# The turned part of the latent heads' keys: two zero-padded tiles of 128 rows in place of one of twice 64 rows

## The chip, the cores and the metric

The kernel runs on one core of a Trainium2 chip, in one launch. Time is the device time of a whole execution in microseconds (us), the median over several runs. A profiled execution has a time of its own; its span runs from the first instruction to the last.

The engines are named as in the profile: PE multiplies matrices (PEld is its loading of weights, which runs beside the multiplying), DVE and ACT work elementwise, POOL too, and SP issues the transfers.

## What is computed

One step of a two-layer transformer for two groups of 128 tokens each, a prompt and a sample; the sample also sees a cache of 128 tokens. The first layer has eight latent heads (multi-head latent attention) and eight grouped-query heads, the second differential attention; each layer has a gated feed-forward part with a convolution of width 3, and modulation vectors from a condition. What matters here is the latent heads. Their key has two parts: 128 features of the head's own, made from a compressed vector, and 64 features that all eight heads share, which are turned by the token's position (rotary embedding):

```python
k_rope = apply_rope(k_rope[:, :, None, :], cos_r, sin_r)[:, :, 0]
krope_all = jnp.concatenate([ctx[1], k_rope], axis=1)
kv = (ckv_all @ w_kv_up).reshape(b, s, MLA_HEADS, MLA_NOPE_DIM + MLA_V_DIM)
ka = jnp.concatenate(
    [kv[..., :MLA_NOPE_DIM], jnp.broadcast_to(krope_all[:, :, None, :], (b, s, MLA_HEADS, MLA_ROPE_DIM))],
    axis=-1)
out_a = softmax_attention(jnp.concatenate([qa_nope, qa_rope], axis=-1), ka, va, MLA_SCALE)
```

A score is therefore a sum over 128 + 64 features. For the prompt there is no cache and no turn.

## The kernel before

**Layout.** Features stand on the 128 rows (partitions) of a tile, tokens along the columns: columns 0 to 127 are the prompt (group 0), then the sample. Keys have three such blocks: prompt, cache, sample. Weights come as blocks of 128 x 128 from memory in transfers of 1 MB (`raw`) and are split by ACT into a rounded high part (`wh`, line 220) and by DVE into the rest (`wl`, line 221); each product is then three matmuls (lines 313, 314, 317). Scores, transposes and attention sums are plain fp32 matmuls, which PE executes in two steps each.

**The turned key.** The weights are arranged so that the 64 shared features are computed twice: row 10 of `pr` (the product of the input with `w_in_ab`, tile name proj) holds them on rows 0 to 63 and again on rows 64 to 127. The cached ones arrive doubled in the same way. The tile `kr` has 128 rows and the three blocks of 128 columns:

- `caches()` (lines 647 to 653) loads the cached block, among the other caches, at the start of the last quarter of the input product (about 142 us).
- `key_rope()` (line 696), started once product 10 of that quarter is done (about 197 us), copies the prompt's block on ACT (line 697), sends it out as a result (line 698) and turns the sample's block on DVE straight into `kr` (line 699; `rope` has four quarter-row products, line 584, and two steps over all rows, lines 586 and 587).

**The queries' turned part.** `qr` is one tile for two heads: the even head's 64 features on rows 0 to 63, the odd head's on rows 64 to 127.

**The heads.** In the loop over `h`, PE makes the queries of two heads (three products) every second round, and in every round the head's keys `kn` and values. A grouped-query head and a latent head are started as generators: `head_ab` first puts the scores into one bank, then the softmax runs on DVE and ACT, and at later calls of `pump` come the transposes of the probabilities (`transposed`, line 607) and the sums (lines 631 to 633). Between these, PE has the products of the following heads and the modulation's rows (`sum_rows`, line 427, with 32 columns of weights). A latent head's scores take four matmuls: for each group the product with `kn` over 128 rows, then that with `kr` over the head's 64 rows:

```python
half = slice(64 * (h % 2), 64 * (h % 2) + 64)
return head_ab(hp, [(qnh, knh), (qrh[half], kr[half])], rsm,
               lambda b: vh[:, b], o, h)
```

A grouped-query head has one product for each group and so two matmuls (`kg`, `qb`).

**What sets the order.** The program is written as one stream and a scheduler places it on the engines; each engine then runs its list strictly in order, and waits are semaphores. Some transfers, those of the caches among them, are kept in the order of the program. Tiles of a pool lie one behind another in the order of their first use: behind `kr` in the pool `ab` stand `kg`, `vg`, `ql`, `qb` and the rest.

Of the kernel before, what the change touches and what calls it, by code (L numbers as in the profile page):

```python
# [18 lines left out]
P = 128  # L19
D = 2048  # L20
KD = D // P
T = 128
# [62 lines left out]
def step_kernel(ctx: ExitStack, tc: tile.TileContext, A: dict):  # L85
    nc = tc.nc
    pe, dve, act, pool, sp = nc.tensor, nc.vector, nc.scalar, nc.gpsimd, nc.sync
# [16 lines left out]
    def nm(s):  # L104
        uid[0] += 1
        return f"{s}_{uid[0]}"

    def T_(pl, shape, tag, dt=F32, bufs=None):
        kw = {} if bufs is None else {"bufs": bufs}
        return pl.tile(shape, dt, tag=tag, name=nm(tag), **kw)  # L110
# [8 lines left out]
    def C(name):  # L119
        a, w = _AT[name]  # L120
        return cst[:, a:a + w]
# [454 lines left out]
    def rope(dst, src, heads, half, cn, sn):  # L576

        cb = C(cn)[:, None, :].to_broadcast([P, heads, T])
        sn_ = C(sn)
        t = T_(tmp, [P, 2, T], "rope", bufs=1)  # L580
        for a in range(0, P, 2 * half):
            lo, hi = slice(a, a + half), slice(a + half, a + 2 * half)
            for to, of in ((hi, lo), (lo, hi)):
                dve.tensor_tensor(out=t[to, :heads], in0=src[of],
                                  in1=sn_[of, None, :].to_broadcast([half, heads, T]), op=ALU.mult)
        dve.tensor_tensor(out=dst, in0=src, in1=cb, op=ALU.mult)
        dve.tensor_tensor(out=dst, in0=dst, in1=t[:, :heads], op=ALU.add)
# [16 lines left out]
    def transposed(pl, p):  # L604
        pt = T_(ppool["att"], [P, 512], "att", bufs=3)
        for b in range(3):
            pe.transpose(pt[:, b * T:(b + 1) * T], p[:, b * T:(b + 1) * T], ident)  # L607
        o = T_(pl, [P, 3 * T], "pT", bufs=2)
        act.copy(o, pt[:, :3 * T])
        return o  # L610

    def head_ab(pl, pairs, rs, v, hx, c):

        s = T_(ppool["att"], [P, 512], "att", bufs=3)
        for g, ks in ((0, slice(0, T)), (1, slice(T, 3 * T))):
            for i, (q, k) in enumerate(pairs):
                pe.matmul(s[:, ks], q[:, g * T:(g + 1) * T], k[:, ks],  # L617
                          start=(i == 0), stop=(i == len(pairs) - 1))
        mx = T_(small, [P, 2], "mx")
        sums = T_(small, [P, 2], "sums")  # L620
        p = T_(pl, [P, 3 * T], "p", bufs=2)
        softmax_parts(s, mx, sums, rs, None, p)
        rec = T_(small, [P, 2], "rec")
        dve.reciprocal(out=rec, in_=sums)
        dve.tensor_scalar(out=p[:, :T], in0=p[:, :T], scalar1=rec[:, 0:1], scalar2=None, op0=ALU.mult)
        dve.tensor_scalar(out=p[:, T:], in0=p[:, T:], scalar1=rec[:, 1:2], scalar2=None, op0=ALU.mult)
        yield
        pT = transposed(pl, p)
        yield
        o = T_(ppool["att"], [P, 512], "att", bufs=3)  # L630
        pe.matmul(o[:, 0:T], v(0), pT[:, 0:T], start=True, stop=True)
        pe.matmul(o[:, T:NT], v(1), pT[:, T:2 * T], start=True, stop=False)
        pe.matmul(o[:, T:NT], v(2), pT[:, 2 * T:], start=False, stop=True)
        split(hx[:, c, :NT], hx[:, c, NT:2 * NT], o[:, :NT])


    def mixer_ab(hx, rb0, st):
        l = 0
        with tc.tile_pool(name="ab", bufs=1) as ab:
            with tc.tile_pool(name="abp", bufs=1) as pj:  # L640
                T_(ab, [P, SHIFT // 4], "pad")
                kv_in = T_(ab, [P, 4, 2, 3 * T], "kv_in", F32R)
                ckc = T_(pj, [P, 4, T], "ckc")
                kr = T_(ab, [P, 3 * T], "kr")
                kg = T_(ab, [P, 2, 3 * T], "kg")
                vg = T_(ab, [P, 3, 2, P], "vg")

                def caches():
                    tc.keep_in_program_order(sp.dma_start(out=ckc, in_=A["cache_ckv"]))
                    split(kv_in[:, :, 0, T:2 * T], kv_in[:, :, 1, T:2 * T], ckc)  # L650
                    tc.keep_in_program_order(sp.dma_start(out=kr[:, T:2 * T], in_=A["cache_krope"]))
                    tc.keep_in_program_order(sp.dma_start(out=kg[:, :, T:2 * T], in_=A["cache_gqa_k"]))
                    tc.keep_in_program_order(sp.dma_start(out=vg[:, 1], in_=A["cache_gqa_v"]))

# [4 lines left out]
                rsm = T_(ab, [P, 2], "rsmla")  # L659
                pr = T_(pj, [P, 15, NT], "proj")  # L660
# [33 lines left out]
                        sp.dma_start(out=A["o_ckv"], in_=ck[:, :, 0:T])  # L694

                def key_rope():
                    act.copy(kr[:, 0:T], pr[:, 10, 0:T])
                    sp.dma_start(out=A["o_krope"], in_=kr[0:64, 0:T])
                    rope(kr[:, None, 2 * T:], pr[:, 10:11, T:], 1, 32, "rcm", "rsm")
                    yield  # L700

                def keys(c):
# [88 lines left out]
            with tc.tile_pool(name="abh", bufs=1) as hp:  # L791
                ada["pew"] = PEW["heads"]

                o = T_(keep, [P, KD, ROW], "hx", F32R)
                load_cw(0)
                WQ = Weights(A["w_q_up"], 6, 2)
                WK = Weights(A["w_kv_up"], 4, 4)
                qh, qlo = (lambda k: ql[:, k, :NT]), (lambda k: ql[:, k, NT:])
                kh, klo = (lambda k: kv_in[:, k, 0]), (lambda k: kv_in[:, k, 1])
                qn, qr = {}, None  # L800

                def gqa_query(h):
                    s2 = T_(tmp, [P, NT], "sq", bufs=2)
                    act.activation(s2, qb[:, h], AF.Square)
                    act.activation(qb[:, h], qb[:, h], AF.Identity, scale=C("gqn"))
                    yield
                    pst = T_(pmisc, [P, 512], "misc")
                    for g in range(2):
                        pe.matmul(pst[:, g:g + 1], s2[:, g * T:(g + 1) * T], inv(128),
                                  start=True, stop=True)  # L810
                    rstd([pst[:, 0:2]], 2, HEAD_SCALE, rsb[:, h])
                    rope(qb[:, h:h + 1, T:], qb[:, h:h + 1, T:], 1, 64, "rch", "rsh")

                def gqa(h):
                    k = kg[:, h // 4]
                    return head_ab(hp, [(qb[:, h], k)], rsb[:, h], lambda b: vg[:, b, h // 4], o, 8 + h)

                def mla(h, qnh, qrh, knh, vh):
                    half = slice(64 * (h % 2), 64 * (h % 2) + 64)
                    return head_ab(hp, [(qnh, knh), (qrh[half], kr[half])], rsm,  # L820
                                   lambda b: vh[:, b], o, h)

                flush()
                start(gqa_query(0))
                for h in range(8):
                    if h % 2 == 0:
                        for i in range(2):
                            ps = gemm(WQ.chunk(), qh, qlo)
                            qn[h + i] = T_(hp, [P, NT], "qn", bufs=4)
                            act.copy(qn[h + i], ps)  # L830
                            pump(RATE["heads"])
                        ps = gemm(WQ.chunk(), qh, qlo)
                        ev = T_(tmp, [P, NT], "nt", bufs=4)
                        act.copy(ev, ps)
                        qr = T_(hp, [P, NT], "qr", bufs=2)
                        act.copy(qr[:, 0:T], ev[:, 0:T])
                        rope(qr[:, None, T:], ev[:, None, T:], 1, 32, "rcm", "rsm")
                        pump(RATE["heads"])
                    if h < 7:
                        start(gqa_query(h + 1))  # L840
                    start(gqa(h))
                    ps = gemm(WK.chunk(), kh, klo, 3 * T)
                    kn = T_(hp, [P, 3 * T], "kn", bufs=2)
                    act.copy(kn, ps)
                    pump(RATE["heads"])
                    ps = gemm(WK.chunk(), kh, klo, 3 * T)
                    vt = T_(hp, [P, 3 * T], "vt", bufs=2)
                    act.copy(vt, ps)
                    pump(RATE["heads"])

                    def values_and_head(h, vt, *a):
                        pt = T_(ppool["att"], [P, 512], "att", bufs=3)
                        for b in range(3):
                            pe.transpose(pt[:, b * T:(b + 1) * T], vt[:, b * T:(b + 1) * T], ident)
                        vm = T_(hp, [P, 3, P], "vm", bufs=2)
                        act.copy(vm.rearrange("p b d -> p (b d)"), pt[:, :3 * T])
                        yield
                        yield from mla(h, *a, vm)

                    start(values_and_head(h, vt, qn[h], qr, kn))  # L860
                flush()
# [370 lines left out]
```

## Time and profile before

| what | value |
| --- | --- |
| median of 3 runs | 2375.56 us (2375.53 to 2375.99) |
| profiled execution | 2375.77 us |
| its span | 2374.0 us, mean granted clock 0.989 |
| first and last scores of the latent heads | 246.5 and 363.5 us |
| their stage, from the first score of a grouped-query head | 228.0 to 363.6 us |
| memory traffic over the span | 257 GB/s on average |

How to read a row of the views. A group of instructions names line, engine, operation, tiles as written<-read, the form (for PE, rows*columns of the array, then rows x columns of the moving tile) and the count, then busy time and mean duration. In a timeline a row has its start, its duration and, in brackets, the idle time of its engine before it and what ended that. PE's matmuls are pipelined, so its rows overlap: what a matmul costs is the distance from its start to the next start, not its duration. An x2 is two steps merged into one row.

### The profile page before, as it was taken

The page shows a single profiled execution, that of the slowest core. Times are in us where ns is not written, and L with a number is a line of the kernel's source. Part 1 is how long each engine was busy: PE and PEld are TensorE (multiplying, and loading weights), DVE is VectorE, ACT ScalarE, POOL GpSimd, SP SyncE. Part 2 cuts the span into 40 slices and gives each one's busy share as a digit, 9 for nine tenths or more (in the row PEclk, how much of TensorE's full clock was granted, in tenths as well). Part 3 has the DMA queues.
Part 4 walks back from the last instruction along what each step waited for, and adds up shares of the span by engine and source line. Part 5 has one row for each costly group of instructions (what it writes and reads, how often), then busy time and mean ns, then how long its engine had stood idle before and what let it go on. Part 6 is the DMA issues. An engine that isn't in the chain of part 4 may idle for free.

```text
span 2374.0 us, 47094 instructions
## 1 busy us (share of the span) xinstructions
PE 2315.6 (98%) x19626; PEld 2196.9 (93%) x19626; DVE 1799.1 (76%) x2677; ACT 1172.7 (49%) x1855; POOL 136.6 (6%) x132
## 2 busy tenths in 40 slices
PE   8899999999999999999999999998999999999997
PEld 6778868799999999999989999897999999999997
DVE  2667544479999999999968889799899755666654
ACT  4345544365554345554465555445555434555542
POOL 0001001110000000001220000022000000000011
PEclk9999999999999999999999999998999999999998
DMA  9886677877767876777767788776677555555553
GB/s 378 353 342 241 238 266 300 309 275 266 261 252 281 296 277 251 265 264 268 300 229 256 267 315 290 269 288 240 247 260 260 207 195 195 196 194 192 192 192 120
DMA packets 92405, 610.81 MB, mean 257 GB/s; under 512 B 9952, under 2 KB 17824, under 8 KB 20512
## 3 DMA queue, kind: packets, MB, share of 16 engines
q1 hardware_dynamic: 92192, 607.80, 69.6%
q8 instruction: 154, 2.52, 0.4%
q14 instruction: 59, 0.48, 0.1%
HBM read 603.01 MB, written 4.75 MB: 256 GB/s over the span
## 4 chain that ended last, share of the span: by engine, by line
PE 95%; DVE 2%; DMA 1%; issue 1%; ACT 1%; POOL 0%; POOLq 0%; DVEq 0%; ACTq 0%
PE acc L313 28%; PE acc L317 28%; PE acc L314 28%; PE ada L427 3%; DMA araw<-w_ada 1%; PE att L617 1%; PE acc L300 1%; PE acc L299 1%; PE acc L301 1%; PE misc L427 0%; PE att L934 0%; PE att L607 0%; DVE wl L221 0%; PE ada L340 0%; PE ada L376 0%
## 5 line engine op out<-in xcount | busy, mean ns | idle before, releaser
L220 ACT CAST wh<-raw 128x1024 fp32r<-128x1024 f32 (+1 forms) x788 | 794.0, 1013 | 943.1 <-PE acc L314 775.7
L221 DVE TENSOR_TENSOR wl<-raw,wh 128x1024 fp32r<-128x1024 f32 (+1 forms) x788 | 923.0, 1186 | 343.8 <-ACT wh L220 324.5
L313 PE MATMUL acc<-hx,wh 128*128 128x256 f32 x4064 | 1131.6, 279 | 9.7 <-ACT wh L220 4.2
L317 PE MATMUL acc<-hx,wl 128*128 128x256 f32 x4064 | 1127.8, 278 | 0.7 <-DVE wl L221 0.7
L314 PE MATMUL acc<-hx,wh 128*128 128x256 f32 x4064 | 1128.4, 278 | 0.0
L313 PEld LDWEIGHTS acc<-hx,wh 128*128 128x128 f32 x4064 | 764.7, 188 | 35.7 <-issue 13.3
L317 PEld LDWEIGHTS acc<-hx,wl 128*128 128x128 f32 x4064 | 765.0, 188 | 8.9 <-issue 6.7
L314 PEld LDWEIGHTS acc<-hx,wh 128*128 128x128 f32 x4064 | 765.3, 188 | 7.4 <-issue 6.9
L404 DVE CUSTOM_DVE_ANT_0 junk<-araw,condb 128x2048 f32<-128x2048 f32 (+1 forms) x184 | 424.8, 2309 | 1.1 <-DMA araw<-w_ada 1.1
L314 PE MATMUL acc<-g,wh 128*128 128x256 f32 x1408 | 388.3, 276 | 0.0
L317 PE MATMUL acc<-g,wl 128*128 128x256 f32 x1408 | 388.0, 276 | 0.0
L313 PE MATMUL acc<-g,wh 128*128 128x256 f32 x1408 | 387.8, 276 | 0.0
L314 PEld LDWEIGHTS acc<-g,wh 128*128 128x128 f32 x1408 | 264.3, 188 | 0.0
L317 PEld LDWEIGHTS acc<-g,wl 128*128 128x128 f32 x1408 | 264.2, 188 | 0.0
L313 PEld LDWEIGHTS acc<-g,wh 128*128 128x128 f32 x1408 | 264.1, 188 | 0.0
L175 POOL TENSOR_TENSOR sqacc<-sqacc,sq 128x256 f32<-128x256 f32 x62 | 80.7, 1302 | 1584.3 <-issue 1290.8
L1011 ACT ACTIVATE cv<-acc,convw 128x256 f32<-128x256 f32 x176 | 98.3, 559 | 2.8 <-PE acc L301 2.8
L569 DVE SCALAR_TENSOR_TENSOR x<-acc,mod,x 128x128 f32<-128x128 f32 x192 | 58.0, 343 | 49.2 <-PE acc L317 49.2
L427 PE MATMUL ada<-araw,condw 128*32 128x512 f32 x608 | 83.2, 624 | 6.0 <-DMA araw<-w_ada 5.0
L1017 DVE SCALAR_TENSOR_TENSOR cv<-acc,convw,cv 128x254 f32<-128x254 f32 x176 | 84.4, 480 | 3.7
L1014 DVE SCALAR_TENSOR_TENSOR cv<-acc,convw,cv 128x254 f32<-128x254 f32 x176 | 83.7, 476 | 2.2 <-ACT cv L1011 2.2
L313 PE MATMUL acc<-oall,wh 128*128 128x256 f32 x208 | 58.4, 281 | 2.3 <-DVE x L569 2.3
(229 smaller groups left out, 1789.8 us busy)
## 6 DMA issues: line engine op xcount, KB each, us to landing
araw<-w_ada SPq DMA_DIRECT2D x186, 1024.0 KB, 5.4
raw<-w_up SPq DMA_DIRECT2D x176, 1024.0 KB, 4.8
raw<-w_down SPq DMA_DIRECT2D x88, 1024.0 KB, 4.8
raw<-w_in_c SPq DMA_DIRECT2D x48, 1024.0 KB, 5.5
raw<-w_in_ab SPq DMA_DIRECT2D x19, 1024.0 KB, 7.1
raw<-w_out_ab SPq DMA_DIRECT2D x16, 1024.0 KB, 7.1
raw<-w_out_c SPq DMA_DIRECT2D x16, 1024.0 KB, 5.3
raw<-w_ada SPq DMA_DIRECT2D x6, 1024.0 KB, 10.8
```

What stands on the lines that cost most here:

```text
L175: pool.tensor_tensor(out=st["acc"], in0=st["acc"], in1=sq, op=ALU.add)
L220: pin(act.copy(out_hi, src))
L221: pin(dve.tensor_tensor(out=out_lo, in0=src, in1=out_hi.bitcast(F32), op=ALU.subtract))
L313: fixed(pe.matmul(ps[:, :n], wh, xh(k), start=(i == 0), stop=False))
L314: fixed(pe.matmul(ps[:, :n], wh, xl(k), start=False, stop=False))
L317: fixed(pe.matmul(ps[:, :n], wl, xh(k), start=False, stop=(i == last)))
L404: tc.keep_in_program_order(dve.tensor_tensor_reduce(out=junk, in0=raw, in1=condb[:, c].rearrange("p (g n) -> p g n", g=4), scale=1.0, scal ...
L427: i = pe.matmul(ada["ps"][32 * g:32 * g + 32, :], condw[:, 4 * t + g, :], raw[:, g], start=(t == 0), stop=(t == 3), skip_group_check=True)
L569: dve.scalar_tensor_tensor(out=x[:, c, s], in0=ps[:, s], scalar=mod[:, l, 3 * which + 2, c, g:g + 1], in1=x[:, c, s], op0=ALU.mult, op1=AL ...
L1011: pin(act.activation(y, ps, AF.Identity, scale=cw[:, 1, m:m + 1], bias=cw[:, 3, m:m + 1]))
L1014: pin(dve.scalar_tensor_tensor(out=y3[:, :, 1:], in0=p3[:, :, :T - 1], scalar=cw[:, 0, m:m + 1], in1=y3[:, :, 1:], op0=ALU.mult, op1=ALU.add))
L1017: pin(dve.scalar_tensor_tensor(out=y3[:, :, :T - 1], in0=p3[:, :, 1:], scalar=cw[:, 2, m:m + 1], in1=y3[:, :, :T - 1], op0=ALU.mult, op1=A ...
```

## The change

`kr` becomes two tiles side by side, each of 128 rows: in the first, rows 0 to 63 hold the shared features and rows 64 to 127 are zero; in the second it is the other way round. POOL clears both once. Each half is filled separately: two transfers for the cached block, two copies on ACT for the prompt's, and the turn goes into a tile of its own (`turned`), from which two more copies on ACT fill the sample's block. In the scores, the whole of `qr` meets the tile of the head's parity: the other head's features meet zeros. The sums are the same.

```diff
-                kr = T_(ab, [P, 3 * T], "kr")
+                kr = T_(ab, [P, 2, 3 * T], "kr")
+                pool.memset(kr, 0.0)
+                halves = (slice(0, 64), slice(64, P))
...
-                    tc.keep_in_program_order(sp.dma_start(out=kr[:, T:2 * T], in_=A["cache_krope"]))
+                    for i, half in enumerate(halves):
+                        tc.keep_in_program_order(sp.dma_start(out=kr[half, i, T:2 * T], in_=A["cache_krope"][half]))
...
                 def key_rope():
-                    act.copy(kr[:, 0:T], pr[:, 10, 0:T])
-                    sp.dma_start(out=A["o_krope"], in_=kr[0:64, 0:T])
-                    rope(kr[:, None, 2 * T:], pr[:, 10:11, T:], 1, 32, "rcm", "rsm")
+                    for i, half in enumerate(halves):
+                        act.copy(kr[half, i, 0:T], pr[half, 10, 0:T])
+                    sp.dma_start(out=A["o_krope"], in_=kr[0:64, 0, 0:T])
+                    turned = T_(pj, [P, 1, T], "turned")
+                    rope(turned, pr[:, 10:11, T:], 1, 32, "rcm", "rsm")
+                    for i, half in enumerate(halves):
+                        act.copy(kr[half, i, 2 * T:], turned[half, 0])
                     yield
...
                 def mla(h, qnh, qrh, knh, vh):
-                    half = slice(64 * (h % 2), 64 * (h % 2) + 64)
-                    return head_ab(hp, [(qnh, knh), (qrh[half], kr[half])], rsm,
+                    return head_ab(hp, [(qnh, knh), (qrh, kr[:, h % 2])], rsm,
                                    lambda b: vh[:, b], o, h)
```

On PE and DVE the lists keep their instructions and their order. ACT, SP and POOL get a few more. ACT around the key's copies, before (line 697 copies the prompt's block, 220 rounds weights, 704 squares the grouped-query keys):

```order
L171 ACTIVATE sq_2036<-proj_240 128x256
L697 COPY kr_233<-proj_240 128x128
L220 CAST wh_2246<-raw_2240 128x1024
L704 ACTIVATE sq_2088<-proj_240 128x256
L704 ACTIVATE sq_2124<-proj_240 128x256
```

and of the change (lines 701 and 706 are the two pairs of copies, 711 is the former 704):

```order
L171 ACTIVATE sq_2038<-proj_241 128x256
L701 COPY kr_233<-proj_241 64x128 x2
L220 CAST wh_2252<-raw_2246 128x1024
L706 COPY kr_233<-turned_2061 64x128 x2
L711 ACTIVATE sq_2094<-proj_241 128x256
L711 ACTIVATE sq_2130<-proj_241 128x256
```

The second pair stands behind the rounding of weights and ahead of the squares; it waits for DVE's turn. SP around the cached block, before (lines 649 to 653 are the caches, 445 the modulation's weights, 265 the layer's weights):

```order
L649 DMA ckc_232<-cache_ckv 128x512
L651 DMA kr_233<-cache_krope 128x128
L445 DMA araw_1501<-w_ada 128x2048
L652 DMA kg_234<-cache_gqa_k 128x2x128
L653 DMA vg_235<-cache_gqa_v 128x256
L265 DMA raw_1799<-w_in_ab 128x2048
```

and of the change (lines 651 to 656 are the caches):

```order
L651 DMA ckc_232<-cache_ckv 128x512
L654 DMA kr_233<-cache_krope 64x128
L445 DMA araw_1502<-w_ada 128x2048
L654 DMA kr_233<-cache_krope 64x128
L655 DMA kg_235<-cache_gqa_k 128x2x128
L656 DMA vg_236<-cache_gqa_v 128x256
L265 DMA raw_1801<-w_in_ab 128x2048
```

The second half stands behind a transfer of modulation weights, ahead of the other caches and the next weights.

## Prediction

> **What bounds the kernel now.** I read the page first, then the busy times of the stage that the change touches, then PE's waits there, then single rows. On the page, the busy line and the chain that ended last:
>
> ```profile
> PE 2315.6 (98%) x19626; PEld 2196.9 (93%) x19626; DVE 1799.1 (76%) x2677; ACT 1172.7 (49%) x1855; POOL 136.6 (6%) x132
> ...
> PE 95%; DVE 2%; DMA 1%; issue 1%; ACT 1%; POOL 0%; POOLq 0%; DVEq 0%; ACTq 0%
> ```
>
> PE holds 95% of the chain: what PE is spared, where it does not wait for another, comes off the end. The stretches (start:end, length, then busy time of PE, PEld, DVE, ACT, POOL with their instructions, granted clock, DMA share, GB/s): the attention heads stand in the first, the output product behind them in the second.
>
> ```profile
> 228.00:363.60 135.60, 133.67 (x919) 102.02 (x918) 66.04 (x199) 69.80 (x164) 4.90 (x7) 1.00 0.69 258
> 380.00:400.00 20.00, 20.00 (x171) 17.11 (x170) 9.89 (x16) 7.85 (x10) 4.96 (x5) 1.00 0.99 397
> ```
>
> In the heads PE works 133.67 of 135.60 us at full granted clock; DVE and ACT work about half, DMA 0.69. All 1.9 us of PE's idle time there have these two names (total, times, longest):
>
> ```profile
> PE att L607 <- DVE p L625: 1.4, 2, 0.8
> PE ada L427 <- DVE mod L378: 0.5, 1, 0.5
> ```
>
> So this is a PE stage, and the question is what the scores cost on PE beyond their columns. The instructions of the score line, durations as minimum/median/maximum, first and last start:
>
> ```profile
> L617 PEld LDWEIGHTS att<-kn,qn x32: 186/189/192, 246.5 to 362.6; 128*128 128x128 f32 x32
> L617 PEld LDWEIGHTS att<-kr,qr x32: 182/184/186, 246.9 to 363.3; 64*128 64x128 f32 x32
> L617 PE MATMUL att<-kr,qr x32: 272/374/480, 246.9 to 363.5; 64*128 64x128 f32 x16, 64*128 64x256 f32 x16
> ```
>
> The 32 kr matmuls run with the array in the form 64*128: two fp32 steps for each of 16 matmuls, in 8 heads. A weight load takes as long with 64 rows (184 ns) as with 128 (189), so nothing is saved now by half the rows. The second latent head, PE in order of time:
>
> ```profile
> 259.03 0.39 PE L633 MATMUL att<-pT,vm 128*128 128x128 f32 x2
> 259.26 0.39 PE L617 MATMUL att<-kn,qn 128*128 128x128 f32 x2
> 259.57 0.49 PE L617 MATMUL att<-kr,qr 64*128 64x128 f32 x2
> 259.99 0.70 PE L617 MATMUL att<-kn,qn 128*128 128x256 f32 x2
> 260.62 0.70 PE L617 MATMUL att<-kr,qr 64*128 64x256 f32 x2
> 261.24 0.44 PE L317 MATMUL acc<-kv_in,wl 128*128 128x384 f32 x1
> 261.52 0.34 PE L313 MATMUL acc<-kv_in,wh 128*128 128x384 f32 x1
> 261.69 0.34 PE L314 MATMUL acc<-kv_in,wh 128*128 128x384 f32 x1
> ```
>
> Durations overlap in this view; the distance from start to start is the cost. L633, a pair of 128 columns in one array form, takes 259.26-259.03 = 0.23 us. The pairs that touch kr take 0.31, 0.42, 0.63 and 0.62, and the instruction behind them, 384 columns, takes 0.28 where its like takes 0.17. For the 256-column pair without a change of form, a grouped-query head, whose four steps are one such pair of each width:
>
> ```profile
> 343.29 0.82 PE L617 MATMUL att<-kg,qb 128*128 128x128 f32 x4
> 343.94 0.60 PE L376 MATMUL ada<-cst,am 128*128 128x128 f32 x4
> ```
>
> All four take 0.65; less 0.22 for the narrow pair, the wide one takes 0.43. The same surcharge stands where PE comes from the 128*32 form of the modulation rows:
>
> ```profile
> 245.48 1.07 PE L427 MATMUL ada<-araw,condw 128*32 128x512 f32 x8
> 246.48 0.49 PE L617 MATMUL att<-kn,qn 128*128 128x128 f32 x2
> 246.90 0.48 PE L617 MATMUL att<-kr,qr 64*128 64x128 f32 x2
> ```
>
> Here the first kn pair takes 0.42 instead of 0.31. So each change of form costs about 0.1 us on each side of it, 0.2 in all, and a latent head makes four: into kr, out, into, out.
>
> **The change, part by part.**
>
> The *scores* keep their number, columns and order; kr's matmuls become 128*128. A head then costs two narrow pairs at 0.22 and two wide ones at 0.43 to 0.44: 1.30 to 1.32 us instead of 261.24-259.26 = 1.98, which saves 0.66 to 0.68; the instruction behind goes from 0.28 to 0.17, another 0.11. Together 0.77 us, eight heads 6.2 us. What stays is the change out of 128*32 ahead of the scores, since those rows are not touched. The zero rows cost nothing in columns. Bounds: at least nothing (if the surcharge is of another cause, below), at most 6.2 plus the 1.9 us of waits.
>
> *What is given back.* The softmax runs from the scores' end on DVE and ACT, and PE fills that time with products whose length does not change, except that the first is 0.11 shorter. Where PE already waits for p, the wait grows. PE first, then DVE, at the sixth latent head:
>
> ```profile
> 340.52 0.28 PE L317 MATMUL acc<-hx,wl 128*128 128x256 f32 x1
> 340.89 0.70 PE L607 MATMUL att<-cst,p 128*128 128x128 f32 x3
> ```
> ```profile
> 338.36 0.29 DVE L593 TENSOR_REDUCE mx<-att 128x1 f32<-128x128 f32 x1 [2.28 <-PE att L617]
> 340.55 0.28 DVE L625 TENSOR_SCALAR p<-p,rec 128x128 f32<-128x128 f32 x1
> ```
>
> PE is free at 340.80, p is done at 340.83, PE starts at 340.89. The chain from 338.36 to 340.83 keeps its length, so of this head's gain 0.2 to 0.3 us (the shorter first product, and a score end that moves less than PE's free time) becomes wait. The other two long waits hang on grouped-query scores or on the modulation's reduction, which move along with PE. I take 0.3: net 5.9.
>
> *Key rows.* ACT's one copy of 128 rows becomes two of 64, and two more copies follow behind the turn on DVE. ACT there, then DVE's last step of the turn, then a 64-row copy of another stage:
>
> ```profile
> 197.56 0.30 ACT L697 COPY kr<-proj 128x128 f32<-128x128 f32 x1 [1.78 <-DVE proj L753]
> 198.35 1.05 ACT L220 CAST wh<-raw 128x1024 fp32r<-128x1024 f32 x1 [0.49 <-PE acc L314]
> 199.88 0.42 ACT L704 ACTIVATE sq<-proj 128x256 f32<-128x256 f32 x1 [0.48 <-DVE proj L753]
> ```
> ```profile
> 199.07 0.29 DVE L587 TENSOR_TENSOR kr<-kr,rope 128x128 f32<-128x128 f32 x1
> ```
> ```profile
> L905 ACT COPY dsh<-acc x32: 257/258/260, 1228.2 to 1500.6; 64x128 f32<-64x128 f32 x32
> ```
>
> The first pair ends at 197.56+2x0.26 = 198.08, before the cast's own release at 198.35. The second pair waits for DVE at 199.36; the cast ahead of it ends at 199.40, so the new wait adds nothing, and both copies end by 199.92. Queued behind them is the square at 199.88: 0.04 late, with PE's products between it and its reader. Cost nothing; without this cover three copies, 0.8 us. DVE's turn keeps its instructions and only writes another tile.
>
> *Queues.* SP gets one more small transfer, behind a modulation load. SP's issues there:
>
> ```profile
> 142.68 1.30 SPq L651 DMA_DIRECT2D kr<-cache_krope  x1
> 145.23 0.68 SPq L653 DMA_DIRECT2D vg<-cache_gqa_v  x1
> 148.46 0.33 SPq L265 DMA_DIRECT2D raw<-w_in_ab  x1
> ```
>
> An issue takes 0.7 to 1.3 us; SP is done at 145.91 and the next weight load leaves at 148.46, so 2.5 us of room hide it. The cached values leave up to 1.3 later and are read only in the heads. Beyond that room it would delay a weight load by the excess; below nothing is excluded, since nothing is taken off the queue but the length of one issue. POOL clears kr once, at the start:
>
> ```profile
> 0.73 0.53 POOL L135 MEMSET condw<- 128x512 f32 x1 [0.29 <-POOLq L1213]
> 20.81 0.70 POOL L187 TENSOR_TENSOR rr<-rv,cst 128x2 f32<-128x2 f32 x1 [19.55 <-DVE rv L183]
> ```
>
> By the row of 512 elements, 768 take 0.8 us, inside 19.55 us of idle time; the first kr transfer waits for it at 142, long after.
>
> *Places.* The larger kr moves the tiles behind it in its pool, the queries' ql among them. No row shows reads by address; the nearest are two gemms on tiles at different places:
>
> ```profile
> L313 PE MATMUL acc<-g,wh 128*128 128x256 f32 x1408 | 387.8, 276 | 0.0
> L313 PE MATMUL acc<-oall,wh 128*128 128x256 f32 x208 | 58.4, 281 | 2.3 <-DVE x L569 2.3
> ```
>
> 5 ns apart; on the 216 matmuls that read ql (12 products of 18) that is 1.1 us either way. I take 0 and keep 1.1 for the range.
>
> **Sum.** 6.2 - 0.3 = 5.9 us. The profiled execution took 2375.77 us, 2374.0 of it span; span 2368.1, execution 2369.9. The median of the runs stands 0.2 below the profiled execution: **2369.7 us**, 0.25% less.
>
> **The rivals.**
>
> *Given back behind the heads.* The output product draws 397 GB/s at a DMA share of 0.99, and the second half of the heads is where PE already waits for p. For it: the waits above. Against it: transfers there are started by freed buffers, which move with PE, and in the stretch from 380 us PE is busy 20.00 of 20.00. If the four heads from 320 us on lose their 0.77 each: 3.1 lost, 2375.56-6.2+3.1 = 2372.5.
>
> *No gain.* The surcharge could belong to the alternation of two products into one bank, not to the form. For it: in the latent heads both come together. Against it: L633 takes other weights and another moving tile than the pair before it, into one bank, at 0.23; and the pair behind 128*32 pays it. Then 2375.6, with 0.2 for late copies 2375.8: within what a measurement of this kernel can tell from no change, 0.2%, or 4.8 us.
>
> *Slower: the weight loads come out of hiding.* Now neighbours differ in their rows; afterwards all loads take all 128. If a load could run under the matmul before it only where the rows differ, each step would pay load plus matmul: 4 x (0.19+0.11) + 4 x (0.19+0.22) = 2.84 us a head against 1.98+0.11 now, 0.75 more, eight times 6.0: 2381.6. It decides as soon as same-row neighbours stand more than the load's 0.19 apart at 128 columns. The L633 row puts them at 0.115, and four kg steps take 0.65, not 1.42: the rows speak against it plainly.
>
> [...]
>
> *More.* The earlier scores could also dissolve the 1.9 us of waits: 2375.56-6.2-1.9 = 2367.5.
>
> **How the numbers follow.** Forecast 0.75 (its own range 2368.6 to 2370.8, from the 1.1 us of places on the near side and the wait's 0.3 doubled on the far one), more 0.04, given back 0.11, no gain 0.07, slower 0.03. The range 2368.0 to 2373.0 holds the forecast and the case given back, 0.86. Faster by over 0.2%: 0.75+0.04 = 0.79; within it 0.11+0.07 = 0.18; slower 0.03. The forecast lies only 1.1 us beyond the 0.2%, so a small loss would turn it into no change.
>
> **What would show it.** In the profile of the changed kernel the score line knows only 128*128; kn and kr pairs start 0.22, 0.22, 0.44 and 0.44 apart, and the product behind them starts at its usual distance. The heads are 5.9 us shorter, PE's wait for p is near 1.7 us, the square behind the key copies is under 0.1 late, and from 400 us on every row stands 5.9 us earlier up to the end. The forecast is wrong if kr pairs still take 0.31 or more in the new form, if the wait for p grows by over 1 us, or if the lead shrinks after 364 us.

## The result and the profile after

| | before | changed |
| --- | --- | --- |
| median, 21 runs each on the same chips | 2375.59 us | 2371.46 us |
| lowest to highest | 2371.74 to 2379.74 | 2366.61 to 2375.46 |
| span of the profiled execution | 2374.0 us | 2368.7 us |

The ratio is 0.9977, with a 95% interval from 0.9971 to 0.9983: 5.5 us less, between 4.0 and 6.9; the plain medians lie 4.1 apart. 2369.7 was forecast, so the changed kernel's median of 2371.46 is 1.8 above it, and the ratio on the 2375.56 of before would give 2370.1. The kernel is faster, and by the ratio just over the 0.2% that the prediction set as the mark between faster and no change; the interval, 0.17 to 0.29% less, doesn't settle that last point.

Single runs of each of the two kernels spread over 8 to 9 us, and those of the changed one go with the mean granted clock (from 2366.61 us at 0.991 to 2375.46 at 0.986), so the reading rests on the stage of the heads, where the clock was 1.00 in both profiles below. It is counted here from the first grouped-query score, at 228.97 us (the stretch from 228.0 ahead of the prediction began 1 us before it), to the first product behind the last latent score. Length, busy times of PE, PEld, DVE, ACT and POOL with their instructions, granted clock, DMA share and GB/s, the kernel before:

```profile
228.97:363.79 134.82, 132.89 (x911) 101.05 (x909) 65.41 (x198) 69.80 (x164) 4.90 (x7) 1.00 0.68 257
```

and the change:

```profile
229.94:359.13 129.19, 126.86 (x911) 101.39 (x910) 65.40 (x199) 69.65 (x164) 4.91 (x7) 1.00 0.72 266
```

The stage is 5.63 us shorter. PE has the same 911 steps and is busy 132.89-126.86 = 6.03 us less; the other engines work as much as before. The score line of the change, weight loads and matmuls of kr:

```profile
L617 PEld LDWEIGHTS att<-kr,qr x32: 190/191/192, 247.7 to 358.9; 128*128 128x128 f32 x32
L617 PE MATMUL att<-kr,qr x32: 275/327/379, 247.8 to 359.1; 128*128 128x128 f32 x16, 128*128 128x256 f32 x16
```

No 64*128 is left, and a load over twice the rows takes 191 ns instead of 184. The second latent head on PE:

```profile
259.53 0.39 PE L617 MATMUL att<-kn,qn 128*128 128x128 f32 x2
259.76 0.39 PE L617 MATMUL att<-kr,qr 128*128 128x128 f32 x2
259.98 0.60 PE L617 MATMUL att<-kn,qn 128*128 128x256 f32 x2
260.41 0.59 PE L617 MATMUL att<-kr,qr 128*128 128x256 f32 x2
260.66 0.53 PE L317 MATMUL acc<-kv_in,wl 128*128 128x384 f32 x1
261.02 0.34 PE L313 MATMUL acc<-kv_in,wh 128*128 128x384 f32 x1
```

Start to start: 0.23, 0.22, 0.43. The last pair and the product behind it share 0.61 (in this view the product starts 0.03 us behind the last step of the pair and stands 0.53 long, where its like has 0.34), read here as 0.44 and 0.17. From the first kn to the second instruction behind the scores it is 1.49 us, where before it was 261.52-259.26 = 2.26: 0.77 a head.

What became of the 0.4 us between 6.03 and 5.63 stands in the waits of the stage and in one row of the sixth latent head:

```profile
PE att L607 <- DVE p L625: 1.6, 3, 0.8
PE ada L427 <- DVE mod L378: 0.5, 1, 0.5
PE ada L427 <- DMA araw<-w_ada: 0.2, 1, 0.2
```
```profile
337.11 0.28 PE L317 MATMUL acc<-hx,wl 128*128 128x256 f32 x1
337.67 0.70 PE L607 MATMUL att<-cst,p 128*128 128x128 f32 x3 [0.28 <-DVE p L625]
```

PE waits for p three times instead of twice; here the 0.09 of before has grown to 0.28. Another 0.2 is a wait for modulation weights, which the stage did not have before.

The preparation, ACT first:

```profile
198.42 0.62 ACT L701 COPY kr<-proj 64x128 f32<-64x128 f32 x2 [1.77 <-DVE proj L760]
199.21 1.05 ACT L220 CAST wh<-raw 128x1024 fp32r<-128x1024 f32 x1 [0.17 <-PE acc L314]
200.26 0.61 ACT L706 COPY kr<-turned 64x128 f32<-64x128 f32 x2
200.89 0.42 ACT L711 ACTIVATE sq<-proj 128x256 f32<-128x256 f32 x1
202.59 0.42 ACT L711 ACTIVATE sq<-proj 128x256 f32<-128x256 f32 x1 [1.29 <-DVE proj L760]
```

A pair of 64-row copies takes 0.62 us. The first fits ahead of the cast, which still waits 0.17 for PE; the second starts as the cast ends, so the turn is not waited for; the square behind it, which had waited 0.48 us before, starts 2.47 us after the first copy, where it was 2.32: 0.15 late. The next square, which had waited 1.44 us for DVE, waits 1.29: the 0.15 is taken up there. SP and POOL:

```profile
144.54 0.51 SPq L654 DMA_DIRECT2D kr<-cache_krope  x1
145.09 0.60 SPq L655 DMA_DIRECT2D kg<-cache_gqa_k  x1
145.74 0.62 SPq L656 DMA_DIRECT2D vg<-cache_gqa_v  x1
149.06 0.33 SPq L265 DMA_DIRECT2D raw<-w_in_ab  x1
```
```profile
1.19 0.74 POOL L645 MEMSET kr<- 128x768 f32 x1
```

SP is done at 146.36 and idle until the next weights leave at 149.06.

### The profile page after: what moved, and what is told of

It is laid out like the page before. It is cut to its first block, busy times and chain, and to the rows that moved or that the text cites. A ratio compares the mean times of both kernels' runs of the same rounds, so it can differ in the third digit from the quotient of the medians.

```text
span 2368.7 us, 47098 instructions
## 1 busy us (share of the span) xinstructions
PE 2308.6 (97%) x19626; PEld 2197.6 (93%) x19626; DVE 1798.8 (76%) x2677; ACT 1173.3 (50%) x1858; POOL 136.0 (6%) x133
## 4 chain that ended last, share of the span: by engine, by line
PE 92%; DVE 3%; DMA 3%; issue 1%; ACT 1%; POOL 0%; POOLq 0%; DVEq 0%; ACTq 0%
PE acc L313 27%; PE acc L317 27%; PE acc L314 27%; PE ada L427 3%; DMA araw<-w_ada 2%; DVE wl L221 1%; PE acc L300 1%; PE acc L299 1%; DVE junk L404 1%; PE acc L301 1%; PE att L617 1%; PE misc L427 1%; PE att L940 0%; PE ada L340 0%; PE att L607 0%
```

## The experiments

Each profile gives the length of the same stage and PE's busy time in it. "Changes" counts how often the scores of the eight latent heads take PE from 128*128 to 64*128 or back.

| kernel | changes | stage, us | PE busy, us | ratio to before (95%) |
| --- | --- | --- | --- | --- |
| before | 32 | 134.82 | 132.89 | |
| the change | 0 | 129.19 | 126.86 | 0.9977 (0.9971 to 0.9983) |
| the change again | 0 | 129.53 | 126.86 | 0.9975 (0.9966 to 0.9984) |
| prep_only | 32 | 134.86 | 132.89 | 1.0000 (0.9992 to 1.0009) |
| grouped | 16 | 131.90 | 129.79 | 0.9989 (0.9980 to 0.9997) |
| mirrored | 16 | 131.90 | 129.81 | 0.9988 (0.9979 to 0.9997) |
| even_only | 16 | 131.84 | 129.76 | 0.9984 (0.9959 to 1.0009) |
| six_changes | 48 | 138.46 | 136.36 | 1.0015 (1.0006 to 1.0024) |
| six_padded | 0 | 129.90 | 127.41 | 0.9981 (0.9962 to 1.0001) |

**prep_only: the new layout without its use.**

```diff
-                    return head_ab(hp, [(qnh, knh), (qrh, kr[:, h % 2])], rsm,
+                    half = slice(64 * (h % 2), 64 * (h % 2) + 64)
+                    return head_ab(hp, [(qnh, knh), (qrh[half], kr[half, h % 2])], rsm,
```

> Both padded key tiles, their clearing, the extra copies and transfer and the moved tiles as in the change, but each score multiplies only the head's 64 rows, as before. Theory (the gain is the change of PE's array form alone): no gain, ratio 1.000 within 0.001; kr rows 64*128, pairs 0.31, 0.42, 0.63, 0.62 apart as before, heads stage as long as before. Rival (the new layout or the moved tiles do the work): most of the 0.23% appears here, ratio near 0.998. Rival (the preparation costs something that the change hides in its net): ratio up to 1.0004, since three copies are 0.8 us.

The ratio is 1.0000 and the stage 134.86 us, PE's busy time in it the same to 0.01:

```profile
230.97:365.83 134.86, 132.89 (x911) 101.03 (x909) 65.40 (x198) 69.71 (x164) 4.89 (x7) 1.00 0.69 257
```

So neither the larger kr nor the tiles that it moves change the heads, and clearing, copies and transfer cost nothing that these runs can tell (the interval leaves at most 0.09%, 2.1 us). The gain of the stage lies in the scores' operands alone.

**grouped: both kn products first, then both kr products.** On the kernel before:

```diff
-        for g, ks in ((0, slice(0, T)), (1, slice(T, 3 * T))):
-            for i, (q, k) in enumerate(pairs):
+        for i, (q, k) in enumerate(pairs):
+            for g, ks in ((0, slice(0, T)), (1, slice(T, 3 * T))):
                 pe.matmul(s[:, ks], q[:, g * T:(g + 1) * T], k[:, ks],
-                          start=(i == 0), stop=(i == len(pairs) - 1))
+                          start=(i == 0), stop=(i == len(pairs) - 1), skip_group_check=True)
```

> The kernel before, with only the order of a latent head's four score matmuls changed: both products with kn first, then both with kr over 64 rows. Theory (each change of form costs 0.2 us): two changes a head in place of four, 0.39 us saved a head, 3.1 us in all, ratio 0.9987; kn to kn and kr to kr pairs at 0.22 and 0.44. Rival (a 64-row matmul is dear by itself): the kr pairs keep their 0.1 us a step, ratio 1.000.

The sample's sum opens in the bank while the prompt's is open; the prompt's scores then lack their kn part (the prompt's result is off by 1.314 of its size; last section), so this kernel computes other scores for the prompt, with the same instructions and columns. The stage came out at 131.90 us, 2.92 less than before; ratio 0.9989. To have the same point with the sums kept, another order followed.

**mirrored: kn, kr, kr, kn.** On the kernel before:

```diff
-            for i, (q, k) in enumerate(pairs):
+            for i, (q, k) in enumerate(pairs[::-1] if g else pairs):
```

> The kernel before, with the sample's two score matmuls in the other order, so that a latent head runs kn, kr, kr, kn and the two products over 64 rows are neighbours. No new tile, copy or transfer. Theory (0.19 us for each change of form): two changes a head instead of four, the stage of the heads near 131.9 us instead of 134.8, ratio 0.9988; between kr and kr 0.22 us as between equal forms. Rival (a product over 64 rows is dear by itself): stage unchanged, ratio 1.000.

Half of the changes gone, half of the gain: 131.90 us, ratio 0.9988. The stage, and its second latent head on PE:

```profile
232.58:364.48 131.90, 129.81 (x911) 101.17 (x910) 65.28 (x198) 69.57 (x164) 4.89 (x7) 1.00 0.70 261
```

```profile
262.43 0.39 PE L617 MATMUL att<-kn,qn 128*128 128x128 f32 x2
262.74 0.92 PE L617 MATMUL att<-kr,qr 64*128 64x128 f32 x4
263.59 0.70 PE L617 MATMUL att<-kn,qn 128*128 128x256 f32 x2
```

The four kr steps, a narrow and a wide pair still over 64 rows, take 0.85 us from start to start; in one form the two pairs take 0.65, and one change into and one out of the form make up the rest, with their other sides on the kn pairs beside them. A product over 64 rows is thus not dear by itself.

**even_only: padding for every second head.**

```diff
-                    return head_ab(hp, [(qnh, knh), (qrh, kr[:, h % 2])], rsm,
+                    half = slice(64 * (h % 2), 64 * (h % 2) + 64) if h % 2 else slice(0, P)
+                    return head_ab(hp, [(qnh, knh), (qrh[half], kr[half, h % 2])], rsm,
```

> As the change, but only the even latent heads multiply the padded 128 rows; the odd ones take their 64 rows. Theory (a fixed price a head, 0.77 us, whichever half of the rows it uses): four of eight heads gain, 3.1 us less than before, ratio 0.9987, even heads' scores 1.12 to 1.13 us long in PE's starts and odd ones 1.98. Rival (the second half of the rows, 64 to 127, is the dear one, since the array is addressed from the middle): under 0.5 us saved, ratio above 0.9995.

The stage is 131.84 us, 2.98 less. The interval of its whole runs is too wide to tell half of the gain from all of it or from none; the stage tells it. The odd heads kept their old starts, here the second latent head:

```profile
259.04 0.39 PE L617 MATMUL att<-kn,qn 128*128 128x128 f32 x2
259.35 0.48 PE L617 MATMUL att<-kr,qr 64*128 64x128 f32 x2
259.77 0.70 PE L617 MATMUL att<-kn,qn 128*128 128x256 f32 x2
260.40 0.70 PE L617 MATMUL att<-kr,qr 64*128 64x256 f32 x2
261.02 0.44 PE L317 MATMUL acc<-kv_in,wl 128*128 128x384 f32 x1
```

That is 1.98 us as before, while the even heads' eight steps took 1.12 to 1.13 in the trace (1.23 behind the 128*32 form). These two lengths can't be subtracted, since the product behind an even head is put early, as in the change. To the second instruction behind the scores it is 2.26 us in this head and 1.49 in the next, 0.77 apart. The heads over rows 0 to 63 are the ones padded here, and they gave the 2.98 us: the price is not one of rows 64 to 127 alone.

**six_changes and six_padded: three alternations a head instead of two.** The same edit on the kernel before and on the change:

```diff
-        for g, ks in ((0, slice(0, T)), (1, slice(T, 3 * T))):
+        cut = ((0, slice(0, T)), (1, slice(T, 3 * T)))
+        if len(pairs) > 1:
+            cut = ((0, slice(0, T)), (1, slice(T, 2 * T)), (1, slice(2 * T, 3 * T)))
+        for g, ks in cut:
```

> The kernel before, with the sample's keys taken block by block (cache, then sample), so that a latent head alternates kn and kr three times instead of twice: the same columns, six changes of form a head instead of four. Theory: two more changes a head at 0.19 to 0.2 us, plus 6 ns for each split matmul step, 3.2 us more in all, ratio 1.0013. Rival (the price is per head or per column, not per change): ratio within 0.0003 of 1.

> The change, with the sample's keys taken block by block, so that kn and kr alternate three times a head, all over 128 rows. Theory: alternating costs nothing without a change of form, so the stage is within 0.2 us of the change's 129.2 (splitting a wide matmul costs 6 ns a step, 8 x 4 steps), ratio to the kernel before 0.9977 like the change. Rival (alternation itself costs, and the padding only halved it): stage 1 to 3.5 us longer than the change's.

The stage of six_changes, then of six_padded:

```profile
231.20:369.66 138.46, 136.36 (x943) 106.09 (x941) 65.62 (x198) 69.84 (x164) 5.02 (x7) 1.00 0.68 253
233.15:363.05 129.90, 127.41 (x944) 102.83 (x942) 65.49 (x199) 69.70 (x164) 5.01 (x7) 1.00 0.72 265
```

With 64 rows the stage grew by 3.64 us to 138.46, ratio 1.0015; behind the first, every pair now stands 0.42 from the next, and all are narrow ones that take 0.22 in one form:

```profile
262.15 0.49 PE L620 MATMUL att<-kr,qr 64*128 64x128 f32 x2
262.56 0.49 PE L620 MATMUL att<-kn,qn 128*128 128x128 f32 x2
262.98 0.48 PE L620 MATMUL att<-kr,qr 64*128 64x128 f32 x2
263.40 0.49 PE L620 MATMUL att<-kn,qn 128*128 128x128 f32 x2
```

Padded, the same alternation costs PE 127.41-126.86 = 0.55 us for 32 more steps, and the stage stands 0.37 to 0.71 above the change's two profiles, more than the 0.2 expected (a split step costs 0.017, not 0.006) but nowhere near the 3.64. The alternation of products is not the price; the change of form is.

**paired_rows: fewer visits to the third form.** The theory says that the modulation's rows, in the form 128*32, pay too. On the change, their two weight tiles are loaded together and multiplied at one visit:

```diff
...
+                ada["pair"] = [T_(wpool, [P, 4, 512], "araw", bufs=2) for _ in range(2)]
+                for n, half in enumerate(ada["pair"]):
+                    sp.dma_start(out=half, in_=A["w_ada"][l, j, q, t + n])
...
         elif pinned[0]:
-            if g == 1 and t:
-                sum_rows(t - 1, ada["last"])
...
+            if t % 2 and g == 3:
...
+                for n in (1, 0):
+                    for c in range(4):
+                        tc.keep_in_program_order(pe.matmul(
...
```

> The change, and the modulation's rows, which use 128*32, summed for two weight tiles at a visit instead of one from the last quarter of the input product on: both tiles are loaded together and the later one is multiplied first. Visits to that form fall from 90 to 67. Theory (each visit pays two changes, 0.33 us by its neighbours' starts): 23 x 0.33 = 7.6 us less than the change, ratio to the kernel before 0.9945, if the bunched loads do not make PE wait. Rival (the loads in pairs come late, PE waits for them at the visits, and other weights queue behind them): waits of PE for the modulation's weights grow from 4.5 us to 10 or more and the gain is lost, ratio 0.998 or above.

It became slower: ratio 1.0072 (1.0042 to 1.0102). Three of its 12 runs, at 2411 to 2419 us, draw this ratio up and stay unexplained; its median, 2386.65, is 15.7 above that of the change on the same chip (2370.98). PE's waits for modulation weights rose to 12.6 us over the whole run, from 4.5+2.8 = 7.3 in the first profile of the change and 6.7+2.7 = 9.4 in the second:

```profile
PE misc L427 <- DMA araw<-w_ada: 7.2, 2, 4.1
...
PE ada L463 <- DMA araw<-w_ada: 5.4, 6, 1.6
```

That is 3.2 to 5.3 us of a loss of some 15 against the change; and the 7.6 less that was expected did not show. Two stretches behind the heads, first of this kernel, then of the change, show where more of it lies:

```profile
356.00:470.00 114.00, 109.16 (x918) 94.18 (x917) 57.22 (x105) 47.15 (x74) 20.30 (x17) 0.99 0.79 303
470.00:520.00 50.00, 40.55 (x302) 32.18 (x302) 26.18 (x53) 23.24 (x43) 4.75 (x6) 0.91 0.73 282
```
```profile
359.00:470.00 111.00, 108.12 (x890) 89.22 (x890) 54.31 (x97) 44.64 (x70) 18.50 (x16) 0.98 0.81 307
470.00:520.00 50.00, 50.00 (x405) 44.48 (x406) 35.70 (x67) 33.90 (x57) 7.25 (x8) 0.94 0.76 288
```

PE idles 14.3 us there instead of 2.9, 6.9 of it in waits for modulation weights. The scheduler also put the list in another order (the stage of the heads is 125.43 us here, but with 863 PE steps in it instead of 911), so the price of a visit to 128*32 stays untested; how the loss splits was not pursued.

**change_again.**

> The change itself on the same chip as the other three. Stage of the heads 129.2 us, ratio 0.997 to 0.998.

Ratio 0.9975, stage 129.53 us, PE busy 126.86 again. None of these kernels was faster than the change.

## Why the prediction was right, step by step

*PE bounds the stage, and the scores pay for changes of form.* Shown. PE's busy time in the stage is linear in the number of changes: (132.89-126.86)/32 = 0.188 us each, (129.80-126.86)/16 = 0.184 (129.80 is the mean of grouped and mirrored; even_only's 129.76 gives 0.181), and from 32 to 48, with the 0.55 of the split steps taken off, (136.36-132.89-0.55)/16 = 0.183. The prediction's 0.77 a head is 0.77/4 = 0.19 a change. Why a change costs this is only in part read off the rows (last section).

*The sum.* 6.2 us gross were forecast, PE's busy time fell by 6.03; 0.3 given back were forecast, 0.40 measured in the first profile (5.63 net) and 0.74 in the second (5.29 net). The ratio's 5.5 lies between, the medians' 4.1 below, as the spread of whole runs allows. The give-back was put at one place, the sixth latent head's wait for p, which has its 0.19; the rest is a wait for modulation weights, 0.2 us in the first profile and 0.5 in the second, which the prediction had not listed. So that the first profile's total came near 0.3 is in part luck. The forecast's own range is worked out loosely too: the wait's 0.3 doubled moves 2369.7 to 2370.0 only, and its far end of 2370.8 stands 1.1 above the forecast, the size of the places.

*Preparation at nothing.* Shown by prep_only within its interval, which leaves up to 2.1 us. The copies were undervalued: 0.31 us each, not the 0.26 of a copy in another stage; the cover ahead of the cast held with 0.17 to spare. The issue times on SP were 0.5 to 0.6 us, and the room there held.

*Places.* The moved tiles were given up to 1.1 us; the stage of prep_only differs by 0.04 from before.

*The rivals.* No gain fell with the change itself and with six_padded, where the alternation stayed and the price was gone. Mirrored takes away alternations and changes of form together, so it can't tell these two apart; it shows that kr's products over 64 rows lose half of the price without padding. The slower one, weight loads that come out of hiding, fell with the change's own rows: kn and kr, all over 128 rows, start 0.11 to 0.115 us a step apart with loads of 0.19. In the kernel before it was the other way round: a load started 0.110 us ahead of its matmul between 128*128 steps, and 0.002 where the form changed (medians, last section). More than the sum did not come either: PE's waits in the stage grew from 1.93 us to 2.33 instead of dissolving. The gain given back behind the heads did not come to 3.1 us: the ratio is that of the stage.

*What failed among the signs.* The square behind the key copies was to be under 0.1 us late and was 0.15 late, because a copy takes 0.31 and not 0.26; the wait of the next square took it up. "From 400 us on every row stands 5.9 us earlier" did not hold row by row. In the two profiles the first score is 229.94-228.97 = 0.97 later, the last one 4.4 earlier, and the end 5.3 earlier. The start is not the change's doing: in mirrored, which prepares nothing, the first score came at 232.58. Whole profiles of one kernel differ by some microseconds before and behind the heads (the change's spans were 2368.7 at a mean granted clock of 0.989 and 2366.8 at 0.991), and this is what the runs' spread looks like from inside. The sign should have been the length of the stage.

## What to carry to other kernels

On PE, look at the form of the array (rows*columns) of neighbouring instructions: here a product over fewer rows paid 0.18 to 0.19 us where its form was entered and as much where it was left, more than the 0.11 that a step of 128 columns takes. If the contraction is short and stands between full ones, zero rows add no columns, and here they took the price away (5.63 us of the stage), with a preparation that fitted into idle time. Putting the short products side by side took half of it without any preparation (mirrored: one line, 0.9988). And judge so small a gain by the length of its stage: here its profiles agree to 0.34 us, where whole runs spread over 8.

## What was unexpected of the hardware

In grouped, the prompt's result is off by 1.314 of its size, and the second layer's keys and values of the prompt by 0.828 and 0.831, while the sample's result stays within 5e-5. The reference with the kn part left out of the prompt's latent scores is off by the same three numbers. So in this kernel, where the second sum opens in the bank between the two products of the first, the later of these replaced what was there, though the columns of the two sums are apart. The run shows this outcome and not what brings it about.

A change of form is paid on both sides: in mirrored the pair ahead of kr is 0.31 instead of 0.22, though it is itself an ordinary 128*128 pair. The weight loads show where. Those of the second latent head, in the kernel before and then in the change:

```profile
259.15 0.30 PEld L617 LDWEIGHTS att<-kn,qn 128*128 128x128 f32 x2
259.57 0.29 PEld L617 LDWEIGHTS att<-kr,qr 64*128 64x128 f32 x2
259.99 0.30 PEld L617 LDWEIGHTS att<-kn,qn 128*128 128x128 f32 x2
```
```profile
259.42 0.30 PEld L617 LDWEIGHTS att<-kn,qn 128*128 128x128 f32 x2
259.65 0.30 PEld L617 LDWEIGHTS att<-kr,qr 128*128 128x128 f32 x2
259.87 0.30 PEld L617 LDWEIGHTS att<-kn,qn 128*128 128x128 f32 x2
```

Where the form stays, a load starts 0.11 us ahead of its matmul and runs under the one before it: 259.15 for 259.26, and in the change 259.42 for 259.53, 259.65 for 259.76 and 259.87 for 259.98. Where the form changes, load and matmul start together, at 259.57 and at 259.99. The whole trace of the kernel before has it so: between 128*128 steps the median lead is 0.110 us, and at the changes, those to and from 128*32 included, it is 0.002. So the first matmul of a form starts late (the first kr 0.31 us behind the start of the kn pair, instead of 0.22), and the step behind it follows later than its columns ask (the kr pair takes 0.42); and the price of a change, 0.18 to 0.19 us, is about the length of one load (0.18 to 0.19). That the uncovered load is the whole price is read from these rows and was not tested by itself; what holds the load back stays open.
